# Wider pace for the token sums of the last four row block pairs

## The chip, the cores and the metric

The kernel runs on one core of a Trainium2 chip. The metric is the device time of one execution in microseconds, with all inputs in HBM at the start and the output in HBM at the end.

## What is computed

A decoder trunk of two layers on 256 tokens of width 2048, all in float32. Each layer is a token mixer (forgetting attention in the first, dilated windows in the second) and a squared ReLU MLP; both add into the residual stream. The change touches the MLPs alone:

```python
def sq_relu_mlp(h, w_up, w_down):
    a = jax.nn.relu(h @ w_up)
    return (a * a) @ w_down

for i in range(DEPTH):
    ...
    h = rms_norm(x, mlp_norm_g[i])
    x = x + sq_relu_mlp(h, mlp_w_up[i], mlp_w_down[i])
```

w_up has 2048 x 8192 elements, w_down 8192 x 2048.

## The kernel before

**Products.** Every float32 operand is split into a high and a low part (wh, wl for weights; hi, lo for activations), and a product of 128 x 512 weights with 128 tokens is three matmuls (lines 447 to 449): high by high, high by low, low by high. A *step* of a normal product is one block of 128 weight rows with both token blocks, so six matmuls. The weights come as tiles of two row blocks (raw, 512 KB, loaded by the SP queue, line 373). One *split* turns such a tile into wh (a cast on ScalarE, line 398) and wl (a subtraction on VectorE, line 399). There are five buffers each for raw, wh and wl. When TensorE has been given the last matmul of split k, the program emits split k + 5, then the load of a raw tile that has come free.

**Strassen slots.** In each MLP a part of h @ w_up (pairs of column blocks named in `WIDE`) is computed by Strassen's scheme with seven products of quarter size instead of eight. For that the kernel needs sums of the token halves of h. h stands transposed, 2048 rows in 16 row blocks of 128, taken in eight *pairs* (pr 0 to 7). For each pair `token_sums` makes the sums on VectorE (lines 592 to 594, in place in a tile called room), casts them to the high part on ScalarE (line 606) and subtracts for the low part on VectorE (line 609). The matmuls of the slots are lines 1138 to 1140. `WIDE_AT` says after how many normal splits each pair's slot is due: for the first column pair after 15, 19, 23, 27, 31, 34, 37 and 39 for pairs 0 to 7. A slot has three *thirds*, each six matmuls with a split of its own: "crossed" (a tile of two raw tiles; VectorE makes the differences sd, line 395, and the sums v, lines 401 and 402), "differences" (which splits sd) and "sums" (which splits v). For pair 0 the third third comes two splits after the first two; for the others one.

**The order on each engine** is that of the program's trace: `Jobs` is a clock of steps. Each six-matmul step is a tick, and a job (a generator) that says `yield n` goes on n ticks later. What a job emits stands in the engine's queue between the splits that were emitted before and after that tick, and `pin` keeps that order. `clear(n)` returns n or n + 1, so that a job goes on in a tick without a split just before it (as far as slots, which turn the parity round, let it). `token_sums` handles one pair after the other: it waits until the pair of h is there, `clear(2)` ticks, the sums, one tick, the casts, one tick, the subtractions. So a pair takes four ticks there. The pairs 0 to 3 are done before the pair 4 begins.

**The beginning of an MLP.** With `b == 0` the column blocks 0 and 1 of w_up are computed as a group (12 row blocks of each, then the last 4 of each), splits 0 to 15. Number the splits of the MLP in their order: 16 and 17 are the first two thirds of the slot of pair 0, 18 and 19 begin column block 2, 20 is the slot's last third, 21 and 22 are normal, 23 and 24 begin the slot of pair 1, 30 and 31 that of pair 2, 37 that of pair 3. When the group's column block is complete, `up_chain` reads its two PSUM tiles by a ReLU on ScalarE (line 1033, tile a_n1a in the first MLP and a_n3a in the second), squares it (line 1037), turns it on VectorE (line 1056) and writes it to DRAM by DMAs that GpSimd issues (line 1050, held); the SP queue reads it back (back, line 354), and ScalarE casts it (line 1081) and VectorE subtracts (lines 1085, 1088). The PSUM tiles that column block 0 leaves are those that column block 2 writes (split 18), and the tiles of column block 1 are those that the slot's last third writes (split 20, wide_n_acc).

Of the kernel before, what the change touches and what calls it, by code (L numbers as in the profile page):

```python
# [119 lines left out]
def trunk(ctx: ExitStack, tc, x, fox_w_in, fox_b_f, fox_q_gain, fox_k_gain, fox_w_out, dil_w_in,  # L120
# [7 lines left out]
    def clear(steps):  # L128

        return steps + (jobs.now + steps + 1 + shift[0]) % 2  # L130
# [453 lines left out]
    def token_sums(tag):  # L584


        for pr in range(KC // 2):
            yield (tag, pr)
            yield clear(2)
            first, second = rooms[tag, pr]  # L590
            a22, a11, a21 = first[:, 1, :], second[:, 0, :], second[:, 1, :]
            nc.vector.tensor_add(a21, a21, a22)
            nc.vector.tensor_sub(a11, a11, a21)
            nc.vector.tensor_add(first, first, a11.unsqueeze(1).to_broadcast([P, 2, P]))
            yield 1
            if pr < KC // 2 - 1:
                hi, lo = (work.tile([P, 4, P], F32R, tag=SUM_TAGS[2 * pr + x], name=f"sums_{tag}_{pr}_{x}", bufs=1)
                          for x in range(2))
                of = [(hi[:, 0:2], lo[:, 0:2], first), (hi[:, 2:4], lo[:, 2:4], second)]
            else:  # L600
                hi, lo, last = (work.tile([P, 3, P], F32R, tag="s", name=f"sums_{tag}_{pr}_{x}", bufs=S_BUFS) for x in range(3))
                of = [(hi[:, 0:2], lo[:, 0:2], first), (hi[:, 2:3], lo[:, 2:3], second[:, 0:1]),
                      (last[:, 0:1], last[:, 1:2], second[:, 1:2])]
            sumT[tag, pr] = [[x[:, i, :] for x in parts for i in range(x.shape[1])] for parts in list(zip(*of))[0:2]]
            for hi, _, whole in of:
                nc.scalar.copy(hi, whole)
            yield 1
            for hi, lo, whole in of:
                nc.vector.tensor_sub(lo, whole, hi.bitcast(F32))
            jobs.done.add(("sums", tag, pr))  # L610
# [536 lines left out]
    def mlp(tag, **after):  # L1147
# [3 lines left out]
        def one(b, n, what, pr):  # L1151
# [13 lines left out]
            slot_steps(tag, banks, what, pr, then)  # L1165

        jobs.spawn(token_sums(tag))
        woven.update(count=0, do=one, due={})
        for at, slot in wide_slots():
# [150 lines left out]
```

## Time and profile before

| | us |
|---|---|
| median of 3 runs | 2093.41 (2092.83 to 2093.63) |
| profiled execution, device time | 2092.2 |
| its span, first to last instruction | 2090.4 |
| PE busy in the span | 2079.0 (99%) |
| DVE busy | 1715.4 (82%) |
| ACT busy | 1306.0 (62%) |
| POOL busy | 275.3 (13%) |

PE is TensorE, DVE is VectorE, ACT is ScalarE, POOL is GpSimd. The times of a timeline are counted from the start of the span. A row of the timeline has start, length, engine, line, operation, written and read tiles, shapes, number of instructions merged, and in brackets the idle time before it with what ended it. The first MLP's tiles have n1 in their names, the second's n3.

### The profile page before, as it was taken

What the parts mean: (1) busy time and instruction counts of PE and PEld (TensorE: products, weight loads), DVE (VectorE), ACT (ScalarE), POOL (GpSimd) and SP (SyncE); (2) the same over time, 40 slices, a digit from 0 to 9 for tenths busy, and PEclk for the clock granted to TensorE, in tenths of its full rate; (3) what the DMA queues carried; (4) which work ended last, traced back from release to release, by engine and by line L of the source; (5) the groups of instructions that cost most, each with busy time, mean ns of one, the idle gap of its engine ahead of it and who ended that gap; (6) DMA issues with size and microseconds to landing.
All of it is one profiled execution on the core that took longest, in us unless ns stands there. A gap on an engine that the chain in (4) does not pass through costs nothing.

```text
span 2090.4 us, 28966 instructions
## 1 busy us (share of the span) xinstructions
PE 2079.0 (99%) x9835; PEld 1820.3 (87%) x9835; DVE 1715.4 (82%) x2183; ACT 1306.0 (62%) x1825; POOL 275.3 (13%) x398
## 2 busy tenths in 40 slices
PE   9999999999999999999999999999999999999999
PEld 7888888888888888888888888888888888888888
DVE  6788876898989889988668787767998898899874
ACT  6665654766666667674656565556766666666662
POOL 2000000021212121120010010000113031212120
PEclk9999999999999999999999999999999999999999
DMA  7888887788888898897977776867788988898885
GB/s 249 256 264 263 258 248 215 249 288 258 271 277 276 257 297 270 266 290 240 287 241 229 250 237 210 265 209 236 241 279 271 283 276 261 278 280 275 267 277 169
DMA packets 357205, 539.04 MB, mean 258 GB/s; under 512 B 43752, under 2 KB 144448, under 8 KB 357056
## 3 DMA queue, kind: packets, MB, share of 16 engines
q1 hardware_dynamic: 334624, 507.41, 75.9%
q0 software_dynamic: 22016, 29.38, 6.2%
q8 instruction: 77, 1.26, 0.2%
q14 instruction: 72, 0.59, 0.1%
q10 hardware_dynamic: 416, 0.39, 0.1%
HBM read 484.09 MB, written 40.39 MB: 251 GB/s over the span
## 4 chain that ended last, share of the span: by engine, by line
PE 92%; DVE 3%; ACT 3%; DMA 1%; issue 1%; SPq 0%; ACTq 0%; DVEq 0%
PE acc L447 24%; PE acc L448 24%; PE acc L449 24%; PE wide_n_tp L1139 2%; PE wide_n_tp L1140 2%; PE wide_n_tp L1138 2%; PE wide_n_acc L1138 2%; PE wide_n_acc L1139 2%; PE wide_n_acc L1140 2%; PE wide_n_sc L1139 2%; PE wide_n_sc L1140 2%; PE wide_n_sc L1138 2%; DVE wl L399 1%; ACT wh L398 1%; ACT room_n L552 1%
## 5 line engine op out<-in xcount | busy, mean ns | idle before, releaser
L399 DVE TENSOR_TENSOR wl<-raw,wh 128x1024 fp32r<-128x1024 f32 (+1 forms) x763 | 919.7, 1214 | 313.3 <-ACT wh L398 304.9
L398 ACT CAST wh<-raw 128x1024 fp32r<-128x1024 f32 (+1 forms) x763 | 786.6, 1045 | 495.0 <-PE acc L449 371.4
L447 PE MATMUL acc<-wh,hT_n 128*128 128x512 f32 x1280 | 487.4, 381 | 1.8 <-ACT a_n1a L1033 0.9
L448 PE MATMUL acc<-wl,hT_n 128*128 128x512 f32 x1280 | 486.2, 380 | 1.3 <-DVE wl L399 1.3
L449 PE MATMUL acc<-wh,hT_n 128*128 128x512 f32 x1280 | 485.6, 379 | 0.0
L447 PEld LDWEIGHTS acc<-wh,hT_n 128*128 128x128 f32 x1280 | 242.5, 189 | 35.8 <-ACT a_n1a L1033 1.3
L448 PEld LDWEIGHTS acc<-wl,hT_n 128*128 128x128 f32 x1280 | 242.5, 189 | 35.2 <-DVE wl L399 2.7
L449 PEld LDWEIGHTS acc<-wh,hT_n 128*128 128x128 f32 x1280 | 242.4, 189 | 34.4
L447 PE MATMUL acc<-wh,aTh_n1a 128*128 128x512 f32 x512 | 194.0, 379 | 0.0
L448 PE MATMUL acc<-wl,aTh_n1a 128*128 128x512 f32 x512 | 194.0, 379 | 0.0
L449 PE MATMUL acc<-wh,aTl_n1a 128*128 128x512 f32 x512 | 194.0, 379 | 0.0
L447 PE MATMUL acc<-wh,aTh_n3a 128*128 128x512 f32 x480 | 181.9, 379 | 0.0
L448 PE MATMUL acc<-wl,aTh_n3a 128*128 128x512 f32 x480 | 181.9, 379 | 0.0
L449 PE MATMUL acc<-wh,aTl_n3a 128*128 128x512 f32 x480 | 181.9, 379 | 0.0
L994 POOL DMA_DIRECT2D x<-y_n x96 | 84.6, 1331 | 480.8 <-ACT y_n L993 422.2
L398 ACT CAST wh<-sd 128x1024 fp32r<-128x1024 f32 x80 | 84.0, 1050 | 97.3 <-DVE sd L395 73.0
L398 ACT CAST wh<-v 128x1024 fp32r<-128x1024 f32 x80 | 84.1, 1052 | 58.2 <-PE acc L449 45.7
L449 PEld LDWEIGHTS acc<-wh,aTl_n1a 128*128 128x128 f32 x512 | 96.8, 189 | 13.8
L447 PEld LDWEIGHTS acc<-wh,aTh_n1a 128*128 128x128 f32 x512 | 96.8, 189 | 13.7
L448 PEld LDWEIGHTS acc<-wl,aTh_n1a 128*128 128x128 f32 x512 | 96.8, 189 | 13.7
L449 PEld LDWEIGHTS acc<-wh,aTl_n3a 128*128 128x128 f32 x480 | 90.7, 189 | 12.9
L448 PEld LDWEIGHTS acc<-wl,aTh_n3a 128*128 128x128 f32 x480 | 90.7, 189 | 12.9
(665 smaller groups left out, 3228.9 us busy)
## 6 DMA issues: line engine op xcount, KB each, us to landing
raw<-in_mlp_w_up_dram SPq DMA_DIRECT2D x296, 512.0 KB, 4.8
raw<-in_mlp_w_down_dram SPq DMA_DIRECT2D x256, 512.0 KB, 5.1
raw<-in_dil_w_in_dram SPq DMA_DIRECT2D x192, 256.0 KB, 3.6
raw<-in_fox_w_in_dram SPq DMA_DIRECT2D x94, 512.0 KB, 4.8
raw<-in_fox_w_out_dram SPq DMA_DIRECT2D x32, 512.0 KB, 5.2
raw<-in_dil_w_in_dram SPq DMA_DIRECT2D x32, 512.0 KB, 5.3
raw<-in_dil_w_out_dram SPq DMA_DIRECT2D x32, 512.0 KB, 4.5
x<-y_n POOLq DMA_DIRECT2D x96, 128.0 KB, 6.3
```

Source lines behind the costliest of these rows:

```text
L398: nc.scalar.copy(hi[:, part, :], raw[:, part, :])
L399: nc.vector.tensor_sub(lo[:, part, :], raw[:, part, :], hi[:, part, :].bitcast(F32))
L447: nc.tensor.matmul(acc[t], ah[:, tok], hi, start=first, stop=False)
L448: nc.tensor.matmul(acc[t], ah[:, tok], lo, start=False, stop=False)
L449: nc.tensor.matmul(acc[t], al[:, tok], hi, start=False, stop=last)
L552: nc.scalar.activation(room[i][:, t, :].rearrange("p (i r) -> p i r", i=4), src, AF.Copy, scale=gc)
L994: nc.gpsimd.dma_start(xt[n][:, t, h * HC:h * HC + HC], y, accum_op=ALU.add)
L1138: nc.tensor.matmul(banks[bank], ah, wh, start=what < 3 and of == 0, stop=False, **alone)
L1139: nc.tensor.matmul(banks[bank], ah, wl, start=False, stop=False, **alone)
L1140: nc.tensor.matmul(banks[bank], al, wh, start=False, stop=of == KC // 2 - 1, **alone)
```

## The change

For pairs 4 to 7 the sums come `clear(6)` ticks after the pair before is done instead of `clear(2)`, and the casts come three ticks after the sums instead of one. The subtractions still come one tick after the casts. Both MLPs go through this function. Nothing else changes: the same instructions, buffers and loads, at other places in the queues of VectorE and ScalarE.

```diff
         for pr in range(KC // 2):
             yield (tag, pr)
-            yield clear(2)
+            yield clear(2 if pr < 4 else 6)
             first, second = rooms[tag, pr]
             a22, a11, a21 = first[:, 1, :], second[:, 0, :], second[:, 1, :]
             nc.vector.tensor_add(a21, a21, a22)
             nc.vector.tensor_sub(a11, a11, a21)
             nc.vector.tensor_add(first, first, a11.unsqueeze(1).to_broadcast([P, 2, P]))
-            yield 1
+            yield 1 if pr < 4 else 3
```

## The prediction

> **What bounds the kernel now.** First the page: busy times, and the clock.
>
> ```profile
> span 2090.4 us, 28966 instructions
> PE 2079.0 (99%) x9835; PEld 1820.3 (87%) x9835; DVE 1715.4 (82%) x2183; ACT 1306.0 (62%) x1825; POOL 275.3 (13%) x398
> PEclk9999999999999999999999999999999999999999
> ```
>
> TensorE is busy nearly all the time, and the last row gives its granted clock as nine tenths or more in every slice. The change takes no matmul away, so it can move the time only by what TensorE waits. Next, therefore, TensorE's waits over the whole run:
>
> ```profile
> PE wide_n_acc L1138 <- ACT a_n1a L1033: 1.6, 1, 1.6
> PE wide_n_acc L1138 <- ACT a_n3a L1033: 1.6, 1, 1.6
> PE acc L448 <- DVE wl L399: 1.3, 2, 0.6
> PE acc L447 <- ACT a_n1a L1033: 0.9, 1, 0.9
> PE acc L447 <- ACT a_n3a L1033: 0.8, 1, 0.8
> ```
>
> Columns: total, times, longest. Besides a start-up wait of 1.5 us these are all. Each MLP has the same three, and the lines place them at its first slot. The timeline of TensorE there:
>
> ```profile
> 408.46 0.38 PE L1138 MATMUL wide_n_tp<-wh,hT_n 128*128 128x512 f32 x1
> ...
> 412.18 0.48 PE L447 MATMUL acc<-wh,hT_n 128*128 128x512 f32 x1 [0.88 <-ACT a_n1a L1033]
> 412.50 0.38 PE L448 MATMUL acc<-wl,hT_n 128*128 128x512 f32 x1
> ...
> 415.90 0.48 PE L448 MATMUL acc<-wl,hT_n 128*128 128x512 f32 x1 [0.65 <-DVE wl L399]
> ...
> 420.11 0.48 PE L1138 MATMUL wide_n_acc<-wh,sums_n 128*128 128x512 f32 x1 [1.56 <-ACT a_n1a L1033]
> 420.43 0.38 PE L1139 MATMUL wide_n_acc<-wl,sums_n 128*128 128x512 f32 x1
> ...
> 429.49 0.38 PE L448 MATMUL acc<-wl,hT_n 128*128 128x512 f32 x1
> ...
> 443.74 0.38 PE L448 MATMUL acc<-wl,hT_n 128*128 128x512 f32 x1
> ...
> 1486.54 0.38 PE L1138 MATMUL wide_n_tp<-wh,hT_n 128*128 128x512 f32 x1
> ...
> 1497.97 0.48 PE L1138 MATMUL wide_n_acc<-wh,sums_n 128*128 128x512 f32 x1 [1.56 <-ACT a_n3a L1033]
> ```
>
> From 429.49 to 443.74 there is no wait and there are 66 matmuls (four normal splits of 12 and three thirds of slots of 6), so one takes 14.25 / 66 = 0.216 us. From the slot's first matmul (408.46) to the first of its last third (420.11) there are 36: two thirds and splits 18 and 19. They should take 7.77 us and take 11.65, so 3.88 are lost; the pitch after the last gap is 0.32 (420.11 to 420.43), 0.10 more. **First MLP 3.98 us. Second: 11.43 less 7.77 plus 0.10, 3.76 us. Together 7.74 us.** Nothing more than that is to be had.
>
> Now who is late. ScalarE in that stretch:
>
> ```profile
> 404.53 0.71 ACT L606 CAST sums_n<-room_n 128x256 fp32r<-128x256 f32 x2 [1.65 <-DVE room_n L594]
> 405.72 1.04 ACT L398 CAST wh<-sd 128x1024 fp32r<-128x1024 f32 x1 [0.48 <-DVE sd L395]
> 406.67 1.04 ACT L398 CAST wh<-raw 128x1024 fp32r<-128x1024 f32 x1
> 410.92 0.71 ACT L606 CAST sums_n<-room_n 128x256 fp32r<-128x256 f32 x2 [3.21 <-DVE room_n L594]
> 411.54 1.08 ACT L1033 ACTIVATE a_n1a<-acc 128x512 f32<-128x512 f32 x2
> 412.51 1.15 ACT L1037 ACTIVATE a_n1a<-a_n1a 128x512 f32<-128x512 f32 x2
> 413.55 1.04 ACT L398 CAST wh<-raw 128x1024 fp32r<-128x1024 f32 x1
> ...
> 416.86 0.80 ACT L606 CAST sums_n<-room_n 128x256 fp32r<-128x256 f32 x3 [1.33 <-DVE room_n L594]
> 417.57 1.99 ACT L398 CAST wh<-raw 128x1024 fp32r<-128x1024 f32 x2
> 419.47 1.07 ACT L1033 ACTIVATE a_n1a<-acc 128x512 f32<-128x512 f32 x2
> ...
> 433.24 0.62 ACT L1081 CAST aTh_n1a<-back_n1a 128x512 fp32r<-128x512 f32 x1 [3.17 <-DMA back_n1a<-held_n1a]
> ```
>
> The casts of the sums (L606, pairs 5, 6 and 7) stand at the head of ScalarE's queue and wait for the sums, 1.65, 3.21 and 1.33 us. Behind the second stands the read of column block 0's PSUM tiles (411.54), for which TensorE waits at 412.18; behind that the cast of split 19 (413.55), for which VectorE and then TensorE wait; behind the third the read of column block 1's tiles (419.47), for which TensorE waits at 420.11. And VectorE:
>
> ```profile
> 401.55 0.75 DVE L609 TENSOR_TENSOR sums_n<-room_n,sums_n 128x256 fp32r<-128x256 f32 x2
> ...
> 409.82 0.29 DVE L592 TENSOR_TENSOR room_n<-room_n,room_n 128x128 f32<-128x128 f32 x1
> ...
> 410.46 0.42 DVE L594 TENSOR_TENSOR room_n<-room_n,room_n 128x256 f32<-128x256 f32 x1
> ...
> 414.62 1.23 DVE L399 TENSOR_TENSOR wl<-raw,wh 128x1024 fp32r<-128x1024 f32 x1 [1.93 <-ACT wh L398]
> ...
> 420.21 0.82 DVE L609 TENSOR_TENSOR sums_n<-room_n,sums_n 128x256 fp32r<-128x256 f32 x3
> 420.94 1.22 DVE L399 TENSOR_TENSOR wl<-raw,wh 128x1024 fp32r<-128x1024 f32 x1
> ...
> 428.04 1.18 DVE L399 TENSOR_TENSOR wl<-raw,wh 128x1024 fp32r<-128x1024 f32 x1
> ...
> 434.84 1.22 DVE L399 TENSOR_TENSOR wl<-raw,wh 128x1024 fp32r<-128x1024 f32 x1 [1.61 <-ACT wh L398]
> ...
> 441.92 1.22 DVE L399 TENSOR_TENSOR wl<-raw,wh 128x1024 fp32r<-128x1024 f32 x1
> ```
>
> The last four subtractions of wl are splits 22, 25, 29 and 32 (counted along the queue). VectorE is the one that is behind, and it then idles 1.93 us for a cast that was held up behind the sums: the two queues hold each other up.
>
> **The change part by part.** A pair costs VectorE 1.06 us for the sums (409.82 to the end of L594 at 410.88) and 0.75 for the subtractions, 1.81; pair 7 0.82 for the subtractions, 1.88. ScalarE pays 0.71 (0.80), and its wait. All is moved, none added; no DMA is issued by this function, and the SP and POOL queues keep their order.
>
> *Where it goes.* I counted ticks by the rules of the job clock. Before, pair 4 has its sums behind split 13 and the rest behind 14, pair 5 behind 15 and 16, pair 6 behind 17 and 18, pair 7 behind 19, 20 and 21. After: pair 4 sums behind 15, casts and subtractions behind 17; pair 5 behind 21 and 23; pair 6 behind 27, casts behind 29, subtractions behind 30; pair 7 behind 34, casts behind 36, subtractions behind 37. The slots take the pairs in order, and split 37 is pair 3's slot, so no slot comes to wait for its sums, no tick is added, and the rest of the order stays.
>
> *First gap.* The tiles must be read by 408.46 + 12 x 0.216 = 411.05. The cast of sd is no later than at 405.72, as VectorE has less ahead of it. Behind it in ScalarE's queue come pair 4's casts (0.71, their sums two splits back, so no wait), the cast of split 18 (1.04) and L1033, two of 1.08: done by 405.72 + 1.04 + 0.71 + 1.04 + 1.08 = 409.6. The gap goes, with 1.4 us to spare.
>
> *Second gap.* From 409.6 L1037 (1.15) and the cast of split 19 (1.04) end at 411.8, and wl (1.23) at 413.0. TensorE asks for it 25 matmuls after 408.46, at 413.9. Gone, with 0.9 to spare.
>
> *Third gap.* Needed by 416.24. The casts of splits 21 and 22 can't go before TensorE is through splits 16 and 17 (five buffers), at 411.05; two casts (1.99) at most and two reads (1.07) behind it: 414.1. Gone, with 2 us.
>
> *What is late next.* After the gaps TensorE comes 3.98 us earlier, and VectorE must follow, with pair 5's subtractions and pair 6 added before split 32. Split 22 ended at 422.16 (420.94 + 1.22). Moved from before it to behind it: pair 5's subtractions, pairs 6 and 7: 0.75 + 1.81 + 1.88 = 4.44, by their rows; instructions overlap at their ends by up to 0.1, so I take 4.1. The idle 1.93 goes too, as its cause does. So split 22 ends at about 416.2; with ScalarE's casts in the way for part of it, 417. Split 25 ended at 429.22 and was wanted at 429.49. It now has 0.75 ahead of it from pair 5 and is wanted at 425.51: split 22 may end at 417.7 at the latest (425.51 - 0.75 - 7.06). Split 32 ended at 443.14, was wanted at 443.74, and has 0.75 + 1.81 more ahead of it: wanted at 439.76, it allows 422.16 + 439.76 - 443.14 - 2.56 = 416.2, and 417.8 if the idle 1.61 at 434.84 goes as well, which is the read-back of column block 0 (L1081, 3.17). That chain starts at L1037, by the bounds above at least 2.9 us earlier (412.51 to 409.6). So TensorE keeps up with 0 to 1 us to spare, and at worst loses 0.8 us in an MLP. Pair 7 comes where the casts of ScalarE wait for TensorE to give buffers back, so its cover is the buffers' depth of four splits.
>
> **The clock.** The gaps, 1.9 us and less with their pitch, cost nothing beyond themselves: the clock's row stays at 9. The Trainium skill (TensorE: Matmul & The Clock Gate, Part 1) says that an idle window of about 3.4 us halves the clock. By it the gaps here are too short, as the trace shows; it matters for the third rival.
>
> **The sum.** 7.74 us less, 0.0 taken back: 2092.2 - 7.7 = 2084.5 for an execution like the profiled one (span 2082.7). The median of the runs is 1.2 above the profiled time, so 2093.4 - 7.7 = **2085.7**; with 0.8 lost in each MLP 2087.3.
>
> **The rivals.** *The read-back does not come earlier* (DMA traffic sets it, not L1037). Then split 29 keeps its start of 434.84, pair 6's subtractions come in on top, and split 32 ends at 443.14 + 0.75 where 439.76 is wanted: 4.1 us, the whole gain, 2093.6. With half of it earlier, 2 us lost in each MLP, 2089.6. For it: 3.17 us of ScalarE's idle were ended by a DMA. Against: that DMA was issued behind weight loads whose issue waits for VectorE, which comes earlier.
>
> *The gaps have another cause than the casts of the sums*, and TensorE waits as before: 2093.4. Against it: what ended the waits is named, and it started the moment that L606 was through.
>
> *VectorE is full where the work goes*, and the time comes out longer:
>
> ```profile
> 435.00:445.00 10.00, 10.00 (x48) 8.77 (x47) 9.96 (x12) 8.13 (x11) 0.00 (x0) 1.00 0.91 316
> ```
>
> The third number with its count is VectorE, busy 9.96 of 10 us. If split 22 still ends at 422.16 and no idle time is won back, split 32 comes 2.56 us later than before with 0.60 in hand: 2.0 us worse than before in each MLP, 2097.4. It decides at the end of split 22: up to about 417 nothing is lost, each us beyond costs about a us, and from 422 on the change loses. Against it: 4.1 us are taken out ahead of that point. By the skill's rule such a wait, six us in one place, would also halve the clock for a window and cost some 1.7 us more in each MLP, an estimate from that page: 2100.8.
>
> **How the numbers follow.** Gaps gone, 0.74 (2085.0 to 2087.3); read-back, 0.14, spread from 2087.3 to 2093.6; other cause, 0.05; VectorE full, 0.07. The range from 2084.8 to 2089.8 takes the first and 0.06 of the second, 0.80. No change is within 0.2%, 4.2 us, about what a measurement of this kernel can tell. Faster than 2089.2: 0.74 and 0.04 of the read-back, 0.78. Same: 0.10 and 0.05, 0.15. Slower: 0.07.
>
> **What would show it.** The waits of TensorE at the slot are gone and its 36 matmuls take 7.8 us; L606 waits for no sums of pairs 4 to 7; L1033 ends by 409.6 and 414.1; split 22 ends before 417.7. I am wrong if waits of TensorE for L399 appear at splits 25 to 35, or if ScalarE still idles before L1033.

## The result and the profile after

| | before | after |
|---|---|---|
| median of six runs each, us | 2092.81 (2091.52 to 2093.63) | 2084.72 (2083.05 to 2085.54) |
| profiled execution, us | 2092.2 | 2084.9 |
| its span, us | 2090.4 | 2083.2 |

The ratio is 0.996, 95% interval 0.9948 to 0.9973: 8.1 us less (5.7 to 10.9 by the interval), where 7.7 were forecast. The time lies 0.08 us below the forecast range of 2084.8 to 2089.8.

The page after, first rows:

```profile
span 2083.2 us, 28968 instructions
PE 2076.8 (100%) x9835; PEld 1818.5 (87%) x9835; DVE 1714.9 (82%) x2183; ACT 1305.8 (63%) x1825; POOL 275.2 (13%) x398
```

VectorE and ScalarE do the same work as before (1715.4 and 1306.0). TensorE's waits after (total, times, longest), all of them:

```profile
PE spare L175 <- DVE zeros L171: 1.5, 1, 1.5
PE acc L448 <- DVE wl L399: 0.5, 2, 0.3
PE ps_g_mix L194 <- POOL x L360: 0.3, 1, 0.3
PE acc L447 <- ACT hT_n L628: 0.2, 1, 0.2
```

The waits for L1033 are gone. Those left are at the start of the kernel and, the two for L399, at 382 and 385 us, ahead of the slot. The timeline of TensorE at both slots:

```profile
408.72 0.38 PE L1138 MATMUL wide_n_tp<-wh,hT_n 128*128 128x512 f32 x1
...
416.49 0.38 PE L1138 MATMUL wide_n_acc<-wh,sums_n 128*128 128x512 f32 x1
...
425.77 0.38 PE L448 MATMUL acc<-wl,hT_n 128*128 128x512 f32 x1
...
440.02 0.38 PE L448 MATMUL acc<-wl,hT_n 128*128 128x512 f32 x1
...
1483.05 0.38 PE L1138 MATMUL wide_n_tp<-wh,hT_n 128*128 128x512 f32 x1
...
1490.82 0.38 PE L1138 MATMUL wide_n_acc<-wh,sums_n 128*128 128x512 f32 x1
```

The 36 matmuls take 7.77 us in both MLPs, where they took 11.65 and 11.43: no gap is left. ScalarE after:

```profile
404.81 1.05 ACT L398 CAST wh<-sd 128x1024 fp32r<-128x1024 f32 x1 [2.59 <-DVE sd L395]
405.76 0.71 ACT L606 CAST sums_n<-room_n 128x256 fp32r<-128x256 f32 x2
...
407.33 1.08 ACT L1033 ACTIVATE a_n1a<-acc 128x512 f32<-128x512 f32 x2
...
413.12 1.08 ACT L1033 ACTIVATE a_n1a<-acc 128x512 f32<-128x512 f32 x2
...
416.11 0.72 ACT L606 CAST sums_n<-room_n 128x256 fp32r<-128x256 f32 x2
...
427.82 0.62 ACT L1081 CAST aTh_n1a<-back_n1a 128x512 fp32r<-128x512 f32 x1 [2.14 <-DMA back_n1a<-held_n1a]
...
429.30 0.70 ACT L606 CAST sums_n<-room_n 128x256 fp32r<-128x256 f32 x2
...
442.70 0.81 ACT L606 CAST sums_n<-room_n 128x256 fp32r<-128x256 f32 x3 [0.53 <-DVE room_n L594]
```

The casts of pairs 4, 5 and 6 (405.76, 416.11, 429.30) start with no wait for their sums. The reads of PSUM come at 407.33 and 413.12 instead of 411.54 and 419.47. Pair 7's casts still wait, 0.53 us, and no wait of TensorE follows. And VectorE, the subtractions of splits 19, 22, 25 and 32:

```profile
410.41 1.23 DVE L399 TENSOR_TENSOR wl<-raw,wh 128x1024 fp32r<-128x1024 f32 x1 [0.28 <-ACT wh L398]
...
415.99 1.22 DVE L399 TENSOR_TENSOR wl<-raw,wh 128x1024 fp32r<-128x1024 f32 x1
...
423.75 1.18 DVE L399 TENSOR_TENSOR wl<-raw,wh 128x1024 fp32r<-128x1024 f32 x1
...
437.59 1.22 DVE L399 TENSOR_TENSOR wl<-raw,wh 128x1024 fp32r<-128x1024 f32 x1
```

VectorE's idle before split 19 fell from 1.93 to 0.28 us. Split 22 ends at 417.21, split 25 at 424.93, 0.84 ahead of TensorE's 425.77, and split 32 at 438.81, 1.21 ahead of 440.02.

### The profile page after: what moved, and what is told of

The parts are those of the page before. It is cut to its first block, busy times and chain, and to the rows that moved or that the text cites. A ratio compares the mean times of both kernels' runs of the same rounds, so it can differ in the third digit from the quotient of the medians.

```text
span 2083.2 us, 28968 instructions
## 1 busy us (share of the span) xinstructions
PE 2076.8 (100%) x9835; PEld 1818.5 (87%) x9835; DVE 1714.9 (82%) x2183; ACT 1305.8 (63%) x1825; POOL 275.2 (13%) x398
## 4 chain that ended last, share of the span: by engine, by line
PE 97%; ACT 1%; DMA 1%; DVE 1%; issue 0%; SPq 0%; ACTq 0%; DVEq 0%
PE acc L448 26%; PE acc L447 26%; PE acc L449 25%; PE wide_n_tp L1139 2%; PE wide_n_tp L1140 2%; PE wide_n_tp L1138 2%; PE wide_n_sc L1139 2%; PE wide_n_acc L1140 2%; PE wide_n_acc L1139 2%; PE wide_n_sc L1140 2%; PE wide_n_sc L1138 2%; PE wide_n_acc L1138 2%; PE sc_d L798 0%; DMA raw<-in_fox_w_in_dram 0%; ACT room_n L552 0%; ACT wh L398 0%
## 5 line engine op out<-in xcount | busy, mean ns | idle before, releaser
L399 DVE TENSOR_TENSOR wl<-raw,wh 128x1024 fp32r<-128x1024 f32 (+1 forms) x763 | 919.5, 1214 | 308.5 <-ACT wh L398 299.3
L447 PEld LDWEIGHTS acc<-wh,aTh_n3a 128*128 128x128 f32 x480 | 90.7, 189 | 12.9
```

Source lines behind the costliest of these rows:

```text
L399: nc.vector.tensor_sub(lo[:, part, :], raw[:, part, :], hi[:, part, :].bitcast(F32))
L447: nc.tensor.matmul(acc[t], ah[:, tok], hi, start=first, stop=False)
```

## The experiments

Each stands against runs of the kernel before on the same chip: 25 runs (median 2092.42) for the first four, 22 runs (2092.12) for the next four, one run for each of the last four. The intervals of the ratios are 2 to 3 us wide to either side, so where a few us decide between two readings, the waits in the trace decide and not the median.

**The pace alone.**

```diff
-            yield 1 if pr < 4 else 3
+            yield 1
```

> The pace alone: clear(6) for pairs 4 to 7, but the casts again one tick behind the sums. Theory (the ledger of the prediction: the casts of the sums at the head of ScalarE's queue hold up the reads behind them, and VectorE's place at split 25 decides what comes next): pair 5's casts still wait for their sums before the read of column block 1's tiles, but VectorE is early enough, so the three gaps are gone and no new wait comes: 7.0 to 7.7 us less than before, as the whole change. Rival A (the distance of the casts is what clears the queue): the third gap stays, 1.8 us in each MLP, so about 4 us less than before.

Measured: 2089.99 (2088.43 to 2093.18), ratio 0.9991 (0.9982 to 1.0), 2.4 us less. Both numbers expected were wrong. The first slot takes 7.77 us, so the three gaps are gone as the theory has it. But the wait came back somewhere else, and the rival had the wrong place. ScalarE, then TensorE, of this kernel:

```profile
437.97 0.80 ACT L606 CAST sums_n<-room_n 128x256 fp32r<-128x256 f32 x3 [2.95 <-DVE room_n L594]
...
441.09 1.07 ACT L1033 ACTIVATE a_n1a<-acc 128x512 f32<-128x512 f32 x2
```

```profile
441.73 0.48 PE L447 MATMUL acc<-wh,hT_n 128*128 128x512 f32 x1 [1.89 <-ACT a_n1a L1033]
```

With casts one tick behind the sums a pair takes eight or nine ticks, and pair 7's casts come to stand ahead of the read of column block 2's tiles. They wait 2.95 us for their sums, and TensorE for the read. It is the same lock (a cast at the head of ScalarE's queue waits for VectorE and holds up the read behind it), one column block later.

**The distance alone.**

```diff
-            yield clear(2 if pr < 4 else 6)
+            yield clear(2)
```

> The distance alone: casts three ticks behind the sums for pairs 4 to 7, the pace as before (a pair then takes six ticks). Theory (ledger): no cast waits for sums any more, so the three gaps go; but pairs 4 and 5 and the sums of pair 6 still stand ahead of split 22 and pair 6's subtractions and pair 7's sums ahead of split 25, so wl of split 25 comes 1.8 us late: TensorE waits 1.8 us for L399 between splits 22 and 25 in each MLP, and the time is about 4 us less than before. Rival B (only the waiting casts matter, VectorE has room): no wait in place of the gaps, 7.7 us less. Rival C (only VectorE's load matters): 0 to 1 us less.

Measured: 2089.71, ratio 0.9987 (0.9978 to 0.9996), 2.7 us less. TensorE's waits:

```profile
PE wide_n_sc L1139 <- DVE wl L399: 2.8, 2, 1.4
PE acc L448 <- DVE wl L399: 0.3, 2, 0.2
```

No wait of TensorE's matmuls for L1033 is listed any more, and in its place stand waits for L399 at splits 24 and 25, which cost 1.65 and 0.43 us in the first MLP, with two losses of a quarter of a us before (at splits 20 and 21): 2.6 us where 1.8 were expected. The loss at split 20 is a last trace of the third gap: there the weight load (PEld) waits for the read of column block 1's tiles, in the first MLP alone. Another thing expected did not come true either. Two of the casts still wait for their sums, and the first stands right ahead of the read of column block 0's tiles:

```profile
416.66 0.19 PEld L1138 LDWEIGHTS wide_n_acc<-wh,sums_n 128*128 128x128 f32 x1 [0.38 <-ACT a_n1a L1033]
```

```profile
409.00 0.71 ACT L606 CAST sums_n<-room_n 128x256 fp32r<-128x256 f32 x2 [1.40 <-DVE room_n L594]
409.62 1.08 ACT L1033 ACTIVATE a_n1a<-acc 128x512 f32<-128x512 f32 x2
...
424.79 0.80 ACT L606 CAST sums_n<-room_n 128x256 fp32r<-128x256 f32 x3 [1.40 <-DVE room_n L594]
```

The read ends at 410.70, before TensorE needs the tiles (12 matmuls behind the slot's start at 408.65, so 411.24). So the distance loosens the lock enough, but VectorE is then too late where the forecast's account of VectorE said it would be. Rival B falls by the waits for L399, rival C because the gaps at L1033 are gone but for a quarter of a us while VectorE is still behind; the interval alone (0.8 to 4.6 us less) would not rule out C.

**The casts freed, the order untouched.** In the kernel before, for pairs 4 to 7:

```diff
-                nc.scalar.copy(hi, whole)
+                nc.scalar.copy(hi, whole if pr < 4 else hT[tag][0][:, 0, 0, 0:hi.shape[1] * P]
+                               .rearrange("p (t n) -> p t n", n=P).bitcast(F32))
```

> The kernel before, its order untouched, but the casts of pairs 4 to 7 read a part of the transposed h that has long been there instead of the sums; the cast does not wait for VectorE (the slots of pairs 4 to 7 thus work on other numbers). VectorE has exactly the work of before at the same places. Theory (ledger): ScalarE's waits of 1.65, 3.21 and 1.33 us go and with them the three gaps and VectorE's idle 1.93, but VectorE has all four pairs ahead of split 22 and ends it at about 420.2 where the changed kernel has 417.2: TensorE waits about 1.8 us in all for L399 from split 20 to 25 in each MLP: about 4 us less than before. Rival B (only the waiting casts matter): 7.7 us less. Rival C (only VectorE's load matters): 0 to 1 us less.

Measured: 2087.96, ratio 0.9977 (0.9967 to 0.9987), 4.5 us less. TensorE's waits, then VectorE's split 22:

```profile
PE acc L448 <- DVE wl L399: 2.0, 6, 0.6
PE wide_n_sc L1139 <- DVE wl L399: 0.5, 2, 0.2
```

```profile
420.04 1.22 DVE L399 TENSOR_TENSOR wl<-raw,wh 128x1024 fp32r<-128x1024 f32 x1
```

This is the cleanest of the runs. VectorE has the work of before in the order of before, ScalarE's casts of pairs 4 to 7 wait for nothing, and all waits for L1033 are gone. Split 22 ends at 421.26 in an execution that reached the slot at 409.56, 1.10 later than the page's; that is 420.2 as expected. What remains is VectorE's lateness: from the slot to split 25, 1.9 us (pitches beyond 0.216: 0.09, 0.83, 0.50, 0.43) where 1.8 were expected. So to open the lock is worth about 4 of the 7.7 us by itself (4.5 by the medians, 4.1 from the first slot on); the rest is to be had only if VectorE has less to do ahead of split 25.

**The changed kernel again.**

> The changed kernel once more, to size the change against the kernel before on one chip, and for a second profiled execution. Theory: the three gaps of both MLPs, 7.7 us less, and single runs of one kernel lie some 2 us apart for reasons outside the slot (the first 45 us and the beginning of the MLP). Rival: the change is worth over 8 us, and there is something besides the gaps that it took away.

Measured: 2084.07 (2082.58 to 2085.11), ratio 0.9961 (0.9949 to 0.9974), 8.35 us less. The profiled executions say where the excess over 7.7 lies. The table gives their time up to the first slot's first matmul, and from there to the end of the span.

| execution | to the first slot | from there to the end |
|---|---|---|
| before, the page's | 408.46 | 1681.9 |
| before, second, third, fourth | 408.07, 408.08, 409.87 | 1682.3, 1682.9, 1681.6 |
| after, the page's | 408.72 | 1674.5 |
| after, second | 406.44 | 1674.5 |

From the first slot on, after is 7.7 us shorter than the mean of before (1682.2). Ahead of the slot the change moves work too (pair 4's sums go from behind split 13 to behind 15), but TensorE's last wait there lies at 387 us or earlier in all of these executions, before any of that work, so it does not show in TensorE's time. Executions of one kernel differ by 1.8 us (before) and 2.3 (after) at the slot. The difference is there early: over all profiled executions of this document TensorE starts its 51st matmul between 13.9 and 16.1 us. What the medians show above 7.7, 0.4 and 0.65, is well within that.

**More work for VectorE at split 24.**

```diff
+            for hi, lo, whole in of * (4 if pr == 5 else 0):
+                nc.vector.tensor_sub(lo, whole, hi.bitcast(F32))
```

> The changed kernel, with pair 5's subtractions made five times instead of once (eight more instructions of 0.34 us on VectorE between splits 23 and 24, in each MLP). In the changed kernel wl of split 24 is 1.26 us and that of split 25 0.83 us ahead of TensorE. Theory (VectorE sets the limit there and nowhere else is room used up): 2.7 us more work less 0.83 in hand gives waits of TensorE for L399 at splits 24 and 25 of 1.9 us together in each MLP, 3.7 us more than the changed kernel, 4 us less than before, and none at split 32. Rival (VectorE has room, the queue of ScalarE alone mattered): the time of the changed kernel, 7.7 to 8.3 us less than before.

Measured: 2088.58, ratio 0.9982 (0.9973 to 0.999), 3.5 us less than before. TensorE's waits (here L1139 has moved to L1141):

```profile
PE wide_n_sc L1141 <- DVE wl L399: 2.5, 2, 1.3
PE acc L448 <- DVE wl L399: 0.5, 3, 0.2
```

At splits 24 and 25 TensorE loses 1.59 and 0.43 us in the first MLP, 2.0 where 1.9 were expected, and nothing at split 32. From the first slot on the execution takes 3.7 us more than the changed kernel, as expected, so the rival falls. The spare time of the changed kernel there is what its rows say, under 1 us.

**Pairs 6 and 7 alone.**

```diff
-            yield clear(2 if pr < 4 else 6)
+            yield clear(2 if pr < 6 else 6)
...
-            yield 1 if pr < 4 else 3
+            yield 1 if pr < 6 else 3
```

> The change for pairs 6 and 7 alone; pairs 4 and 5 as before. Theory (ledger): no cast of pairs 6 and 7 waits ahead of a read of PSUM, so the three gaps go; but ahead of split 25 VectorE has pairs 4, 5 and 6 where the changed kernel has pairs 4 and 5, 1.7 us more with 0.83 in hand: waits of 0.8 to 1.2 us for L399 at splits 22 to 25 in each MLP, 5.5 to 6 us less than before. Rival (only the two pairs whose casts stood ahead of the reads matter): all of the gain, 7.7 us.

Measured: 2085.63, ratio 0.9967 (0.9955 to 0.998), 6.5 us less. The size was near, the place was not:

```profile
PE acc L448 <- DVE wl L399: 0.5, 2, 0.3
```

```profile
440.09 0.48 PE L448 MATMUL acc<-wl,hT_n 128*128 128x512 f32 x1 [0.15 <-DVE wl L399]
...
1500.76 0.48 PE L448 MATMUL acc<-wl,hT_n 128*128 128x512 f32 x1 [0.32 <-DVE wl L399]
```

There is one wait in each MLP: at 440.1 us, which is split 32, in the first (0.42 us lost), and at 1500.8, which is split 25, in the second (0.58). I had counted split 25 alone; pair 7 stands ahead of split 32 in this kernel and behind it in the changed one. The rival is off by these two waits only, 1.0 us together: most of the gain comes from pairs 6 and 7.

**The pace, with the distance for pair 7 alone.**

```diff
-            yield 1 if pr < 4 else 3
+            yield 1 if pr < 7 else 3
```

> The pace of the change for pairs 4 to 7, but the casts three ticks behind the sums for pair 7 alone (with the casts at one tick for all four, pair 7's casts waited 2.95 us for their sums ahead of the read of column block 2's tiles, and TensorE lost 2.2 and 1.7 us there). Theory (a cast that waits costs only where a read of PSUM stands behind it): pair 7's casts now stand behind split 32, wait about 1.5 us at most, and the read comes about when TensorE wants it: a wait of 0 to 0.6 us in each MLP, 6.5 to 7.7 us less than before. Rival (pairs 5 and 6 need the distance too): 2.4 us less than before, as with the pace alone.

Measured: 2085.39, ratio 0.9968 (0.9956 to 0.998), 6.7 us less. TensorE's waits for L1033 fell to

```profile
PE acc L447 <- ACT a_n1a L1033: 0.4, 1, 0.4
PE acc L447 <- ACT a_n3a L1033: 0.4, 1, 0.4
```

which cost 0.7 us each. The rival (pairs 5 and 6 need the distance too) falls. The theory needs one word more, as ScalarE shows:

```profile
411.38 0.71 ACT L606 CAST sums_n<-room_n 128x256 fp32r<-128x256 f32 x2 [1.58 <-DVE room_n L594]
...
413.90 1.07 ACT L1033 ACTIVATE a_n1a<-acc 128x512 f32<-128x512 f32 x2
...
424.69 0.71 ACT L606 CAST sums_n<-room_n 128x256 fp32r<-128x256 f32 x2 [3.33 <-DVE room_n L594]
...
437.18 0.81 ACT L606 CAST sums_n<-room_n 128x256 fp32r<-128x256 f32 x3 [1.47 <-DVE room_n L594]
...
438.85 1.06 ACT L1033 ACTIVATE a_n1a<-acc 128x512 f32<-128x512 f32 x2
```

The longest wait, 3.33 us of pair 6, costs nothing. Pair 5's 1.58 us stands ahead of a read of PSUM and costs nothing either, because the read ends at 414.97 and TensorE wants the tiles at 415.57. Only pair 7's 1.47 us costs. So a cast that waits costs where what stands behind it then ends after TensorE asks for it.

**The kernel before against itself.**

> The kernel before itself: how far two medians of one kernel lie apart, and whether a second profiled execution has the same waits. Expected: within 1 us of the kernel before, and in both MLPs the three gaps of 1.0, 0.8 and 1.7 us.

Measured: 2092.7 beside 2092.12, ratio 1.0 (0.9991 to 1.0009), with the three gaps in both MLPs.

**The pace alone, two more executions.** Its first execution was 4.1 us shorter than the kernel before from the slot on, the medians differ by 2.4.

> The pace alone once more, for a second profiled execution: the first one was the fastest of its 11 runs, and from the first slot to its end it is 4.1 us shorter than the kernel before, where the medians differ by 2.4. Theory: the same wait at column block 2's tiles (2.2 and 1.7 us) and some more behind it. Rival: the stretch behind the first slot is the same within 0.3 us, and the rest of the difference is scatter ahead of it.

> The same kernel a third time, with the same two expectations: the stretch from the first slot to the end longer than in the first execution by over 1 us (theory), or the same within 0.3 us (rival).

Single runs: 2090.08 and 2092.55, beside one of the kernel before, 2091.58. From the first slot to the end they take 1680.3 and 1682.3 us, the first 1678.0: the theory holds. What comes behind the wait shows in TensorE's timeline of the third execution, and in its busy times by window (the last three numbers: granted clock, DMA share, GB/s):

```profile
441.56 0.48 PE L447 MATMUL acc<-wh,hT_n 128*128 128x512 f32 x1 [1.88 <-ACT a_n1a L1033]
...
442.53 0.55 PE L448 MATMUL acc<-wl,hT_n 128*128 128x512 f32 x1
442.87 0.63 PE L449 MATMUL acc<-wh,hT_n 128*128 128x512 f32 x1
443.30 0.63 PE L447 MATMUL acc<-wh,hT_n 128*128 128x512 f32 x1
```

```profile
442.00:445.00 3.00, 3.00 (x10) 2.39 (x9) 3.00 (x5) 3.00 (x5) 0.00 (x0) 0.60 0.59 175
```

About 1 us behind the gap the pitch becomes 0.427 us, twice the usual, until 446.2, and the granted clock of the window falls to 0.60. The same follows the second MLP's gap of this execution (1.9 us of idle) and the first MLP's of the second execution (2.4 us), but not the second MLP's there (1.4), nor either in the first execution (1.9 and 1.4). So this kernel gains 4.1 us from the first slot on where the clock stays whole, 1.9 with one half clock and a gap longer by 0.5, and nothing with two and a gap longer by 0.5.

**The kernel before, for its clock.**

> The kernel before, a third profiled execution. With the pace alone, TensorE's clock fell to half for some 3 us behind its gap in two of three executions (pitch 0.427 us). Theory: the gaps of the kernel before, 1.6 us of idle at most, never lower the clock, so the change is worth 7.7 us and no more. Rival: in some executions they do, and the change saves that as well, 1.6 us each time: then a pitch of 0.427 us shows behind the third gap.

> The kernel before, a fourth profiled execution, with the same two expectations: pitch 0.32 then 0.216 us behind every gap (theory), or 0.427 us for some 3 us behind one (rival).

Single runs: 2092.86 and 2093.19, beside another of the same kernel, 2091.64. In four profiled executions of the kernel before, eight third gaps, the pitch behind each is 0.32 and then 0.216. The mean clock over the whole run was 1.000 in all 25 runs of the kernel before beside the first group, and below that, 0.998 or 0.999, in 9 of the 11 of the pace alone. So most runs of the pace alone seem to pay for a half clock, which fits its median gain of 2.4 us. The change did not save clock, and the theory stands: 7.7 us.

## Why the prediction was right or wrong

*The bound* was right: from the first slot on, the time moved by TensorE's waits at the two first slots and by nothing else. 7.74 us were forecast to go there, 7.7 went.

*The places* were right: in VectorE's queue pair 4's sums stand behind split 15, pair 5's behind 21, pair 6's behind 27 and pair 7's behind 34, as counted.

*The three gaps* went in the order of the working. The first tiles were read by 408.4 (bound 409.6), split 19 was there at 411.6 (413.0), the second tiles at 414.2 (414.1, in an execution that reached the slot 0.26 later). That the lock of the queues was the cause of the waits for L1033 is shown by the freed casts alone.

*What is late next* was right in place and near in size: split 22 at 417.2 where 416.2 to 417 was said (416.95 with the slot's 0.26 taken off), 0.8 and 1.2 us in hand at splits 25 and 32 where 0 to 1 was said. The read-back came 5.4 us earlier (433.24 to 427.82), so the first rival did not arise. The other two did not either.

*One sign was wrong:* casts of pair 7 still wait for sums, 0.53 us.

*The step that failed* is the last term of the sum, and with it the lower end of the range. The mechanism was right; the term was mis-sized. "The median of the runs is 1.2 above the profiled time, so 2093.4 - 7.7" added 1.2 us to the 2084.5 that the trace gave, on the word of three runs. Measured, the median of before lies 0.6 above the profiled 2092.2 (six runs, 2092.81, which include those three; the three new ones are 2091.52, 2091.89 and 2092.79) and 0.2 above it in 25 further runs (2092.42). The median of after lies 0.2 *below* its profiled time (2084.72, 2084.9). So of the 1.0 us between 2085.7 and 2084.72, 0.6 is the level of before, and 0.4 is what the medians show beyond 7.7. That this rest is scatter from ahead of the slot is likely by the table above, but two profiled executions of after do not prove it.

The range had the same hole. Its case "gaps gone, 2085.0 to 2087.3" had bounds for the gaps and for VectorE but none for the stretch ahead of the slot, where single executions lie from 406.4 to 409.9 us. Since the forecast gain was at its ceiling, the spread that was left below came from there. The width went into the upper part, for rivals that took 4 us back. With the level of 25 runs the same working gives 2092.4 - 7.7 = 2084.7. That this is the measured time to 0.1 is luck, as is the side of the bound on which a miss of 0.08 us falls: six runs of one kernel spread over 2 us.

*The clock* was weighed too lightly. The Trainium skill (TensorE: Matmul & The Clock Gate, Part 1) names an idle window of about 3.4 us. For the gaps of the kernel before, 1.57 us at most, the clock stayed whole as said. But with the pace alone the half clock followed the gap of 2.4 us and two of three of 1.9 us. The price put on it, 1.7 us, agrees with the runs (below); the length from which it falls due does not, and here the measurement decides. The third rival would have paid it from a shorter wait on.

## What to carry to other kernels

Look at what stands behind an instruction that waits at the head of a queue: casts of sums that no matmul needed for several slots held up the reads of PSUM for which TensorE waited. To move the producer and its consumer apart and to take the work out of the crowded stretch are two remedies, and here each alone gave a third of the gain by the medians, because the first leaves the other engine late and the second sets the same lock one stage on. When all of a forecast gain is taken from waits that a trace lists, add the scatter of the runs to both ends of the range, and take the level from more than three of them: here single runs of one kernel spread over 3.5 us (25 runs, 2090.5 to 2094.0), nearly half of the gain.

## What the runs showed of the hardware that was not expected

TensorE's clock falls to half behind shorter gaps than expected: idle of 1.9 us did it in two of three cases and 2.4 us in the one there was, idle of 1.57 us or less in none (eight third gaps of the kernel before, two of 1.4 us with the pace alone). The half clock begins 0.3 to 1.3 us after work resumes and lasts 3.41 us (441.98 to 445.40 in the second execution of the pace alone, 442.61 to 446.03 and 1521.22 to 1524.64 in the third). Each time it costs 1.7 us: in the third execution one pitch of 0.34, seven of 0.427 and one of 0.30 instead of nine of 0.216.

Why two of three can be read from the records of the granted clock. In each execution the times between its changes are multiples of 3.413 us (433.49 in the third execution of the pace alone is 127 of them), so its changes fall on the ends of intervals of that length. The three gaps that the half clock followed lie whole in one interval, with 2.38, 1.88 and 1.87 us of idle; each time the half clock is the next interval. The gap of 1.89 us in the first execution of the pace alone lies across an end of an interval, with 1.67 us in one and 0.22 in the next, and the clock stayed whole. So it seems to be the idle inside one interval that counts, and whether a gap near 1.9 us costs more than itself depends on where it falls. The limit is not sharp in these data: behind the last matmul of a kernel 1.90 us of idle in one interval was not followed (the kernel before, fourth execution) and 1.97 was (the freed casts). No run here tests this by moving a gap.

Also, the first matmul behind a gap is followed after 0.32 us instead of 0.216, whatever the gap's length (idle of 0.15 to 2.4 us at the places above).
